# A decoder step on eight cores, rewritten from stages with barriers to 512-token tiles as concurrent threads

## The chip, the cores and the metric

One Trainium2 chip, one program on all 8 cores; each core computes one prompt of 2,048 tokens and four samples of 8 tokens with the same weights. The metric is the device time of the slowest core in microseconds (us). Such a program has a second, slower state in some executions, in which the cores of one die (0 to 3 or 4 to 7), sometimes of both, are granted a lower clock; runs marked slow are not compared.

In the later runs the slow state was so frequent (31 of the 75 runs in the experiments, of the kernel before and of the others alike) that I also compare *undisturbed cores*: of all cores of all runs of one kernel, those whose span is within 1% of that kernel's shortest span. The cores exchange nothing here, so such a core shows the kernel without the slow state. For the kernel before, this median is 3,171, 3,171 and 3,169 us on three chips, so values from different chips may be compared.

## The reference, cut to what matters

```python
def swiglu_ffn(x, w_in, w_out):
    g, u = jnp.split(x @ w_in, 2, axis=-1)
    return (jax.nn.silu(g) * u) @ w_out
# layer 0:  x += 0.5*ffn(rms(x)); x += gla(rms(x)); x += 0.5*ffn(rms(x))
# shared:   k, v = proj(rms(x)); k = rope(rms_per_head(k))
# layer 1:  x += 0.5*ffn(rms(x)); x += dilated_window_attention(rms(x), k, v); x += 0.5*ffn(rms(x))
# D_MODEL 1024, FFN 2688, GLA: 4 heads of 128 x 256 with a per-token decay, state carried from chunk to chunk
# attention: 12 query heads, 4 kv heads of 64, three groups (window, dilation) = (128,1), (512,4), (2048,16)
```

Per core this is four tiles of 512 prompt tokens (two pairs in both kernels) and one group of 32 sample tokens, each through four feed-forward blocks (FFN), one GLA (gated linear attention), one K/V projection and one attention.

## The kernel before

Everything is emitted in one program order. A stage is a list of steps, one per weight slice; every step serves both tiles of a pair (and the sample, in the first pair). The norm of a stage stands at its head, one tile after the other on one buffer, and a barrier of all engines stands at its end.

```python
def norm_to_hT(p, gcol, cvn, piece=512):
    sqb = cvn.bf([128, 8, piece]); rs = cvn.f32([128, piece])      # one buffer each
    ...
    for (c0, n) in pieces:                                        # tile after tile
        S.op(ACT, ... activation(out=sqb[:, :, 0:n], in_=xT[:, :, c0:c0 + n], func=AF.Square))   # 8 x n at once
        mm_group(PS[b][:, 0:n], [(onesb, sqb[:, fc, 0:n]) for fc in range(8)], ...)
        ...                                                       # Ln, Exp(-0.5 ..)
        for fc in range(8): S.op(DVE, ... hT = xT * gain * rs)

def ffn(p, l, f):
    emit_norm = norm_to_hT(...)
    for j in range(21):                       # step: w_in, two strips of 128 columns (512-byte rows)
        for (c0, n) in subs:                  # 512, 512 and (first pair) 32 tokens
            ...                               # 8 + 8 matmuls
            S.op(ACT, ... sg = Silu(PS[bg])); S.op(DVE, ... act = sg * PS[bu])
    for m in range(8): ...                    # step: w_out, 21 matmuls a tile, x += 0.5 * PS
    prefetch_steps(); emit_norm(); run_steps()
    S.barrier()

def gla(p):
    for (c0, n, kind) in tiles:               # one tile after the other, weights loaded for each
        step(ld(2048, 16), fn_g); ...         # gates; then v, q, k, recurrence
        step(None, fn_rec)                    # ends with S.barrier()
        ...                                   # output gates with Silu, output projection, S.barrier()
```

K is normed token by token in fp32 and transposed through the matrix engine; x and y are transposed there too. The sample's attention goes through 16 cache blocks per sequence.

Of the kernel before, what the change touches and what calls it, by code (L numbers as in the profile page):

```python
# [11 lines left out]
ENGS = ("pe", "act", "dve", "pool", "sp")  # L12
EPS = 1e-6
ds = bass.ds
# [3 lines left out]

class Sched:
    def __init__(self, nc):  # L20
        self.nc = nc
        self.sem = {e: nc.alloc_semaphore("prog_" + e) for e in ENGS}
        self.cnt = {e: 0 for e in ENGS}
        self.waited = {e: {} for e in ENGS}
        self.ops = {e: [] for e in ENGS}
        self.lastw = {}
        self.readers = {}
        self.semobj = {self.sem[e].name: self.sem[e] for e in ENGS}
        self.dma_sems = {}

    def _need(self, eng, tok, waits):
        if tok is None:
            return
        sname, val, peng = tok
        if peng == eng and peng == "pe":
            return
        if self.waited[eng].get(sname, 0) >= val:
            return
        waits[sname] = max(waits.get(sname, 0), val)

    def op(self, eng, fn, reads=(), writes=(), dma=None):
        psr = [r for r in reads if isinstance(r, tuple) and r[0] in ("ps", "psbf")]
        if psr:
            reads = [r for r in reads if r not in psr]
            writes = list(writes) + psr
# [7 lines left out]
        for s, v in waits.items():  # L53
            self.waited[eng][s] = v
        if dma is None:
            self.cnt[eng] += 1
            tok = (self.sem[eng].name, self.cnt[eng], eng)
            inc = (self.sem[eng], 1)
        else:
# [6 lines left out]
            tok = (ent[0].name, ent[1], "dma:" + dma)  # L66
# [9 lines left out]
    def barrier(self, skip=("ws", "vg")):  # L76
        for e in ENGS:
            waits = []
            for o in ENGS:
                if o != e and self.cnt[o] > self.waited[e].get(self.sem[o].name, 0):  # L80
                    waits.append((self.sem[o].name, self.cnt[o]))
                    self.waited[e][self.sem[o].name] = self.cnt[o]
            for name, (sm, c) in self.dma_sems.items():
                if name.startswith(skip):
                    continue
                if c > self.waited[e].get(sm.name, 0):
                    waits.append((sm.name, c))
                    self.waited[e][sm.name] = c
            if waits:
                self.ops[e].append((waits, None, None))  # L90

    def final_wait(self, eng="sp"):
# [9 lines left out]
    def emit(self):  # L102
        nc = self.nc
        with nc.Block() as block:
# [9 lines left out]
            block.tensor(mk("pe"))  # L114
            block.scalar(mk("act"))
            block.vector(mk("dve"))
            block.gpsimd(mk("pool"))
            block.sync(mk("sp"))

C_ID, C_LE, C_GE, C_SCP, C_SCS, C_MS, C_SQ, C_SM, C_MN, C_ONE, C_BD, C_RM, C_END = 0, 128, 256, 384, 640, 672, 704, 708, 1116, 1212, 1340, 1468, 1596  # L120
DIL = ((128, 1), (512, 4), (2048, 16))

def build_consts():
    c = np.zeros((128, C_END), np.float32)
    r = np.arange(128)
    c[:, C_ID:C_ID + 128] = np.eye(128)
    c[:, C_LE:C_LE + 128] = (r[:, None] <= r[None, :])
    c[:, C_GE:C_GE + 128] = (r[:, None] >= r[None, :])
    c[:, C_SCP:C_SCP + 256] = 1.0
    c[:, C_SCP] = 0.0  # L130
    c[:, C_SCP + 128] = 0.0
    c[:, C_SCS:C_SCS + 32] = 1.0
    c[:, C_SCS:C_SCS + 32:8] = 0.0
    t = np.arange(32)
    c[:32, C_MS:C_MS + 32] = ((t[:, None] // 8 == t[None, :] // 8) & (t[:, None] <= t[None, :]))
    for s in range(4):
        c[:32, C_SQ + s] = (t // 8 == s)
    for rt in range(17):
        for g, (win, dil) in enumerate(DIL):
            for tq in range(8):  # L140
                col = C_SM + rt * 24 + g * 8 + tq
                if rt < 16:
                    R = rt * 128 + r
                    d = 2048 + tq - R
                    c[:, col] = ((d % dil == 0) & (d >= 0) & (d <= win))
    for s in range(4):
        for g, (win, dil) in enumerate(DIL):
            for tq in range(8):
                col = C_MN + s * 24 + g * 8 + tq
                d = tq - (t % 8)  # L150
                c[:32, col] = ((t // 8 == s) & (d >= 0) & (d % dil == 0))
    c[:, C_ONE:C_ONE + 128] = 1.0
    c[:, C_BD:C_BD + 128] = (r[:, None] // 64 == r[None, :] // 64)
    for m in range(128):
        if m % 64 < 32:
            c[m + 32, C_RM + m] = -1.0
        else:
            c[m - 32, C_RM + m] = 1.0
    return c

def build_rope():
    half = 32
# [3 lines left out]
    return np.stack([np.cos(ang), np.sin(ang)], axis=0).astype(np.float32)  # L166

def build(stage=99, phases=None):
# [8 lines left out]
    xp = din("xp", [2048, 1024]); xs = din("xs", [32, 1024]); st_in = din("st", [16, 128, 256])  # L177
    ck = din("ck", [4, 2048, 256]); cv = din("cv", [4, 2048, 256])
    small = din("small", [64, 128])
    knq = din("knq", [2, 64])  # L180
    ffn_in = din("ffn_w_in", [2, 2, 1024, 5376]); ffn_out = din("ffn_w_out", [2, 2, 2688, 1024])
    gla_in = din("gla_w_in", [1024, 3088]); gla_g2 = din("gla_w_gate2", [16, 512]); gla_out = din("gla_w_out", [1024, 1024])
    kv_w = din("kv_w", [1024, 512]); wq = din("attn_w_q", [1024, 768]); wo = din("attn_w_out", [768, 1024])
    consts = din("consts", [128, C_END]); rope = din("rope", [2, 128, 2080])
    y_p = dout("y_p", [2048, 1024]); y_s = dout("y_s", [32, 1024])
    stp_o = dout("stp", [4, 128, 256]); sts_o = dout("sts", [16, 128, 256])
    kp_o = dout("kp", [2048, 256]); vp_o = dout("vp", [2048, 256]); ks_o = dout("ks", [32, 256]); vs_o = dout("vs", [32, 256])

    S = Sched(nc)
    A = nc.alloc_sbuf_tensor  # L190
    TPM = 1056
    xT = A("xT", [128, 8, TPM], F32)
    hT = A("hT", [128, 8, TPM], BF16)
    NSLOT = 4
    wsl = A("wsl", [128, NSLOT, 4096], BF16)
    CF = A("CF", [128, C_END], F32)
    CB = A("CB", [128, C_END], BF16)
    G = A("G", [128, 64], F32)
    negb = A("negb", [128, 4], F32)
    KNQ = A("KNQ", [128, 2, 64], F32)  # L200
    wg2 = A("wg2", [16, 512], BF16)
    Sst = A("Sst", [128, 4, 256], F32)
    Sbf = A("Sbf", [128, 4, 256], BF16)
    KT = A("KT", [128, 2, 2048], BF16)
    KTs = A("KTs", [128, 2, 32], BF16)
    Vg = A("Vg", [128, 3, 16, 256], BF16)
    Vsn = A("Vsn", [32, 256], BF16)
    zer = A("zer", [128, 512], BF16)
    SCRW = 19100
    scr = A("scr", [128, SCRW], F32)  # L210
    PS = [nc.alloc_psum_tensor(f"ps{b}", [128, 512], F32) for b in range(8)]
    NB = 5
    LL = 5
    PBFS = [PS[6][:, :].bitcast(BF16), PS[7][:, :].bitcast(BF16)]
    bank_ctr = [0]

    bank_ring = [list(range(NB))]

    def newbank():
        ring = bank_ring[0]  # L220
        b = ring[bank_ctr[0] % len(ring)]
        bank_ctr[0] += 1
        return b

    class Carver:
        def __init__(self):
            self.off = 0

        def f32(self, shape):
            n = int(np.prod(shape[1:]))  # L230
            v = scr[:shape[0], self.off:self.off + n]
            self.off += n
            assert self.off <= SCRW, (self.off, SCRW)
            return v if len(shape) == 2 else v.rearrange(_pat(len(shape)), **_dims(shape))

        def bf(self, shape):
            n = int(np.prod(shape[1:]))
            w = (n + 1) // 2
            v = scr[:shape[0], self.off:self.off + w].bitcast(BF16)[:, 0:n]
            self.off += w  # L240
            assert self.off <= SCRW, (self.off, SCRW)
            return v if len(shape) == 2 else v.rearrange(_pat(len(shape)), **_dims(shape))

    def _pat(nd):
        names = "abcd"[:nd - 1]
        return "p (" + " ".join(names) + ") -> p " + " ".join(names)

    def _dims(shape):
        names = "abcd"[:len(shape) - 1]
        return {names[i]: int(shape[i + 1]) for i in range(len(shape) - 2)}  # L250

    SP, PL, ACT, DVE, PE = "sp", "pool", "act", "dve", "pe"
    S.op(SP, lambda e: e.dma_start(out=CF[:], in_=consts[:, :]), writes=["CF"], dma="c0")
    S.op(PL, lambda e: e.dma_start(out=CB[:], in_=consts[:, :]), writes=["CB"], dma="c1")
# [26 lines left out]
    def _rs_init():  # L281
        if "load_idx" in rs_state:
            return
# [947 lines left out]
```

## Time and profile before

| | before |
|---|---|
| time, three runs | 3,183.6 / 3,217.4 / 3,220.5 us |
| span, slowest core of the profiled run | 3,199.2 us |
| PE / ACT / DVE busy | 82% / 24% / 31% |
| granted PE clock by core | 0.878 to 0.890 |
| time of weight queue q0's packets, as share of the 16 engines' span | 58.1% |

PE is the matrix engine, PEld its weight load, ACT the activation engine, DVE the vector engine, POOL and SP issue most transfers. In a line of waits the figures are: total us, number of waits, the longest. In a timeline: start, length, engine, source line, operation, output<-input, shapes, count, and in brackets the idle time before with what ended it. The views that carry the reading are in the prediction.

### The profile page before, as it was taken

To read this page: it belongs to the slowest core of one execution; us is meant where nothing else is said; L and a number is where in the kernel's file an instruction comes from. 1 tells how busy PE (TensorE), PEld (TensorE's weight loads), DVE (VectorE), ACT (ScalarE), POOL (GpSimd) and SP (SyncE) were. 2 spreads that over 40 slices of the span, in tenths; PEclk is the share of its full clock that TensorE was granted. 3 is DMA by queue.
4 is the path that set the end of the run, shared out by engine and by line. 5 is a ranking of instruction groups with operands and counts; after the bars stand their busy time and mean duration, and the time that the engine had idled before them with its cause. 6 is when DMAs were issued, how large, how long until landed. Compare 5 with 4: busy or idle time off the path is not lost.

```text
span 3199.2 us, 43773 instructions; the slowest of 8 cores (3162.7 to 3199.2 us)
## 1 busy us (share of the span) xinstructions
PE 2633.8 (82%) x15479; PEld 1246.8 (39%) x15479; DVE 976.6 (31%) x1843; ACT 761.9 (24%) x1445; POOL 476.9 (15%) x532
## 2 busy tenths in 40 slices
PE   5997775499948995868997998686998599877998
PEld 3443332244423442443444443332443244333444
DVE  3213442321143215643213212443112411265211
ACT  2112331211032104622102111423111311164110
POOL 1210001122003210011210220000220222000220
PEclk9998887599768998759998998897998699987999
DMA  6785468678318863256784795673793389501784
GB/s 108 73 82 62 62 94 121 92 73 80 46 37 79 77 65 53 35 74 82 72 81 101 70 85 54 86 93 43 73 86 46 58 78 90 67 15 17 73 84 88
DMA packets 619875, 228.60 MB, mean 71 GB/s; under 512 B 531648, under 2 KB 613200, under 8 KB 619664
## 3 DMA queue, kind: packets, MB, share of 16 engines
q0 software_dynamic: 602464, 194.61, 58.1%
q1 hardware_dynamic: 17200, 31.20, 3.2%
q8 instruction: 130, 2.13, 0.3%
q14 instruction: 81, 0.66, 0.1%
HBM read 404.94 MB, written 15.40 MB: 131 GB/s over the span
## 4 chain that ended last, share of the span: by engine, by line
PE 74%; DVE 8%; ACT 7%; DMA 6%; issue 3%; POOL 1%; DVEq 0%; ACTq 0%; SPq 0%; POOLq 0%
PE ps L342 69%; DVE hT L441 4%; ACT scr L433 2%; DMA scr<-cv 1%; PE ps L991 1%; DMA wsl<-gla_w_in 1%; PE ps L1023 1%; DMA scr<-xp 1%; DMA sts<-scr 1%; ACT scr L803 1%; DVE scr L563 1%; DMA wsl<-ffn_w_in 1%; DVE scr L1132 1%; ACT scr L439 1%; ACT scr L802 1%
## 5 line engine op out<-in xcount | busy, mean ns | idle before, releaser
L342 PE MATMUL ps<-hT,wsl 128*128 128x512 bf16 (+2 forms) x7720 | 1429.8, 346 | 80.3 <-DVE hT L441 37.8
L342 PEld LDWEIGHTS ps<-hT,wsl 128*128 128x128 bf16 (+1 forms) x7720 | 654.3, 99 | 844.0 <-issue 150.7
L342 PE MATMUL ps<-scr,wsl 128*128 128x512 bf16 (+1 forms) x3920 | 721.3, 345 | 31.8 <-DVE scr L1132 21.0
L471 DVE TENSOR_TENSOR scr<-scr,ps 128x512 bf16<-128x512 f32 (+1 forms) x420 | 239.1, 586 | 934.8 <-PE ps L342 934.6
L342 PEld LDWEIGHTS ps<-scr,wsl 128*128 128x128 bf16 x3920 | 331.3, 99 | 420.4 <-issue 97.9
L299 POOL DMA_DIRECT2D wsl<-ffn_w_in x336 | 294.4, 879 | 1255.1 <-DMA wsl<-ffn_w_in 839.6
L469 ACT ACTIVATE scr<-ps 128x512 f32<-128x512 f32 (+1 forms) x420 | 216.9, 517 | 964.7 <-PE ps L342 964.6
L342 PE MATMUL ps<-scr,CB 128*128 128x512 bf16 (+2 forms) x464 | 145.8, 449 | 291.6 <-ACT scr L433 189.0
L441 DVE SCALAR_TENSOR_TENSOR hT<-xT,G,scr 128x512 bf16<-128x512 f32 (+2 forms) x344 | 196.3, 571 | 195.4 <-ACT scr L439 163.6
L486 DVE SCALAR_TENSOR_TENSOR xT<-ps,xT 128x512 f32<-128x512 f32 x160 | 91.7, 590 | 522.4 <-PE ps L342 522.4
L433 ACT ACTIVATE scr<-xT 128x4096 bf16<-128x4096 f32 (+2 forms) x43 | 105.3, 2449 | 560.0 <-DVE xT L486 472.2
L342 PEld LDWEIGHTS ps<-scr,CB 128*128 128x128 bf16 x464 | 48.8, 121 | 392.9 <-issue 386.9
L299 POOL DMA_DIRECT2D wsl<-ffn_w_out x64 | 89.2, 1394 | 398.4 <-PE ps L342 396.8
L342 PE MATMUL ps<-wsl,hT 128*128 128x512 bf16 (+3 forms) x408 | 92.2, 394 | 17.8 <-ACT scr L333 13.4
L333 ACT COPY scr<-ps 128x512 f32<-128x512 f32 (+4 forms) x59 | 33.3, 583 | 306.0 <-PE ps L408 158.3
L1001 ACT ACTIVATE scr<-ps 128x48 bf16<-128x48 f32 (+4 forms) x318 | 74.8, 290 | 63.7 <-PE ps L991 61.7
L299 POOL DMA_DIRECT2D wsl<-gla_w_in x35 | 30.7, 883 | 332.5 <-PE ps L342 242.7
L342 PEld LDWEIGHTS ps<-wsl,hT 128*128 128x128 bf16 (+1 forms) x408 | 44.2, 111 | 64.8 <-issue 37.6
L1006 DVE TENSOR_TENSOR scr<-scr,CB 128x96 bf16<-128x96 bf16 (+4 forms) x159 | 48.2, 303 | 50.6 <-ACT scr L1001 46.3
L1024 PE MATMUL ps<-scr,CB 128*64 128x24 bf16 (+4 forms) x636 | 56.0, 226 | 0.0
L437 ACT ACTIVATE scr<-ps 128x512 f32<-128x512 f32 (+2 forms) x43 | 19.5, 453 | 136.1 <-DVE hT L441 83.6
L751 DVE SCALAR_TENSOR_TENSOR scr<-scr,G 128x512 bf16<-128x512 f32 (+1 forms) x40 | 26.1, 652 | 67.7 <-ACT scr L748 62.3
(124 smaller groups left out, 1298.6 us busy)
## 6 DMA issues: line engine op xcount, KB each, us to landing
wsl<-ffn_w_in POOLq DMA_DIRECT2D x336, 256.0 KB, 4.9
wsl<-ffn_w_out POOLq DMA_DIRECT2D x64, 672.0 KB, 8.7
wsl<-gla_w_in POOLq DMA_DIRECT2D x30, 1024.0 KB, 12.0
wsl<-gla_w_out POOLq DMA_DIRECT2D x10, 1024.0 KB, 9.8
scr<-xp SPq DMA_DIRECT2D x16, 512.0 KB, 6.8
y_p<-scr SPq DMA_DIRECT2D x16, 512.0 KB, 4.5
scr<-rope SPq DMA_DIRECT2D x8, 512.0 KB, 3.9
scr<-ck POOLq DMA_DIRECT2D x8, 512.0 KB, 8.0
```

What stands on the lines that cost most here:

```text
L299: S.op(PL, (lambda e, o=osl, s_=src: e.dma_start(out=o, in_=s_)), writes=[("ws", sl)], dma=f"ws{sl}_{pi}")
L333: S.op(ACT, lambda e: e.copy(out=out, in_=in_), reads=reads, writes=writes)
L342: ins = e.matmul(out, lhsT=l, rhs=r, start=(start and i == 0), stop=(stop and i == n - 1), skip_group_check=skip)
L433: S.op(ACT, (lambda e, c0=c0, n=n: e.activation(out=sqb[:, :, 0:n], in_=xT[:, :, c0:c0 + n], func=AF.Square)), reads=xkeys(c0, n), writes= ...
L439: S.op(ACT, (lambda e, n=n: e.activation(out=rs[:, 0:n], in_=rs[:, 0:n], func=AF.Exp, scale=-0.5)), reads=["rs"], writes=["rs"])
L441: S.op(DVE, (lambda e, fc=fc, c0=c0, n=n: e.scalar_tensor_tensor(out=hT[:, fc, c0:c0 + n], in0=xT[:, fc, c0:c0 + n], scalar=G[:, gcol + fc ...
L469: S.op(ACT, (lambda e, bg=bg, n=n, sl=sl: e.activation(out=sg[sl][:, 0:n], in_=PS[bg][:, 0:n], func=AF.Silu)), reads=[("ps", bg)], writes= ...
L471: S.op(DVE, (lambda e, bu=bu, n=n, sl=sl, j=j, c0=c0: e.tensor_tensor(out=act[:, j, c0:c0 + n], in0=sg[sl][:, 0:n], in1=PS[bu][:, 0:n], op ...
L486: S.op(DVE, (lambda e, b=b, n=n, m=m, c0=c0: e.scalar_tensor_tensor(out=xT[:, m, c0:c0 + n], in0=PS[b][:, 0:n], scalar=0.5, in1=xT[:, m, c ...
L1001: S.op(ACT, (lambda e, pview=pview, sview=sview: e.activation(out=pview, in_=sview, func=AF.Exp, scale=0.125)), reads=[("ps", bs)], writes ...
L1006: S.op(DVE, lambda e: e.tensor_tensor(out=pall, in0=pall, in1=mask.unsqueeze(1).to_broadcast([r1_ - r0_, 4, nqq]), op=ALU.mult), reads=["C ...
L1024: ins = e.matmul(accD[hp * 64:hp * 64 + 64, j // 2, 0:nqq], lhsT=CB[r0_:r1_, C_ONE:C_ONE + 64], rhs=rhs, start=False, stop=False, skip_gro ...
```

## The change

The intent: keep the matrix engine fed by having several independent chains to choose from. Each tile (and the sample) is a Python generator, "thread", that walks through all stages. Evacuations, recurrences and attention blocks are spawned as further threads. A merger repeatedly takes the operation with the lowest estimated start, ties by rank, and appends it to its engine's program. No stage barrier is left: only semaphores for true dependencies. Weights are laid out by the host so that each unit (1 MB of fp32, 8 KB rows) is contiguous, and stream through one ring of eight such units (bf16); a unit is freed when the sample and both tiles of a pair have used it. Silu becomes Exp, Ln, Exp, so that one activation table serves the whole kernel (one table load in its trace, 26 in the one before). Squares for the next norm are taken as each eighth of x is finished. x, y, K arrive and leave feature-major. The core of the diff:

```diff
-    for j in range(21):
-        ... for (c0, n) in subs: ...
-    prefetch_steps(); emit_norm(); run_steps()
-    S.barrier()
+class Threads:
+    TIE = 0.15
+    def run(self):
+        ...
+            cands = [(S.start_of(th[3][1], th[3][3], th[3][4]), th) for th in self.live if th[3] is not None]
+            m = min(c[0] for c in cands) + self.TIE
+            th = min((c for c in cands if c[0] <= m), key=lambda c: (c[1][0], c[1][1]))[1]
+            S.op(eng, fn, reads, writes, cost, dma, nbytes)
+def c_act(n): return 0.11 + n * 0.00083          # the estimates, us
+def c_dve(n, rate=1): return 0.07 + n / (960.0 * rate)
+    def weights():                                # thread: one ring for all weights, states and caches
+        for k, u in enumerate(order):
+            ...
+            yield need(lambda over=over: all(o.left == 0 for _, _, o in over))
+            yield O(PL, ... dma_start(out=dst, in_=u.src), writes=[u.key] + [o.key for _, _, o in over], ...)
+    def tail(T, m, last):                         # behind each eighth of x
+        ...
+            yield square(T, m); done.add(("sq", T.nm, sqn, m))
+    def ffn(T, f, last):
+        for j in range(NF):
+            u = yield from use(T, "fi%d" % f, j)
+            ...                                   # 8 + 8 matmuls
+            TH.spawn(post(j, bs, g, up), T.rank - 3)   # Exp, Ln, Exp, two multiplies
+    def tile_thread(T, prev):
+        yield from load_x(T, prev)
+        yield from norm(T, 0);  yield from ffn(T, 0, False)
+        yield from norm(T, 8);  yield from (gla(T) if T.n == 512 else gla_s(T))
+        ...
+        yield from norm(T, 40); yield from ffn(T, 3, True)
+    TH.spawn(weights(), -30); ...
+    TH.spawn(tile_thread(tiles[0], None), 0);  TH.spawn(tile_thread(TS, None), TS.rank)      # TS: the sample, rank -20
+    TH.spawn(tile_thread(tiles[1], None), 10); TH.spawn(tile_thread(tiles[2], tiles[0]), 20)
+    TH.spawn(tile_thread(tiles[3], tiles[1]), 30)
```

## The prediction

> **What bounds the kernel now.** I read four views: the page, busy time by stage, the clock core by core, and the waits of the matrix engine. First the page's busy table and slices.
>
> ```profile
> PE 2633.8 (82%) x15479; PEld 1246.8 (39%) x15479; DVE 976.6 (31%) x1843; ACT 761.9 (24%) x1445; POOL 476.9 (15%) x532
> ...
> PE   5997775499948995868997998686998599877998
> ...
> PEclk9998887599768998759998998897998699987999
> ```
>
> PE is the only engine near full, but its row dips about eight times, and the clock row dips with it. So I cut the span at the stages (busy time by stretch, slowest core; last three figures: granted clock, DMA share, GB/s):
>
> ```profile
> core 5: us, PE busy (x) PEld busy (x) DVE busy (x) ACT busy (x) POOL busy (x), PEclk, DMA share, GB/s
> ...
> 330.00:604.00 274.00, 163.77 (x1040) 82.46 (x1040) 94.62 (x182) 73.17 (x129) 21.34 (x25) 0.77 0.63 95
> 604.00:625.00 21.00, 8.58 (x30) 3.02 (x31) 8.11 (x12) 11.16 (x8) 5.86 (x7) 0.58 0.64 63
> ...
> 980.00:1212.00 232.00, 231.53 (x1512) 111.29 (x1510) 47.30 (x99) 30.94 (x66) 45.30 (x47) 0.99 0.72 69
> ...
> 2808.00:2940.00 132.00, 102.43 (x816) 45.45 (x815) 83.03 (x156) 70.91 (x179) 0.00 (x0) 0.82 0.02 5
> ```
>
> The feed-forward stretch (980 to 1212) is solid at clock 0.99. The mixers, norms and K/V stages between are not: 274 us hold 164 us of slow matmul in the first GLA, the norm after it has 9 in 21. Two pieces of the chain that ended last give the rate of a solid stretch:
>
> ```profile
> 979.80 231.75 PE ps L342 x1512
> ...
> 2964.34 216.69 PE ps L342 x992
> ```
>
> The second is 512 columns only: 216.69 / 992 = 218.4 ns each. The first is 1008 of those (220.1 us), which leaves 11.6 us for 504 of 32 columns, 23 ns each. With these rates, and the estimates of the next part for 128 and 256 columns, the program before (9,924 matmuls of 512 columns, 344 of 256, 1,522 of 128, 3,689 smaller) is about 2,380 us of matmul. The other 820 of 3,199 us are PE waiting or at half clock. The waits of PE name who it waits for:
>
> ```profile
> PE ps L342 <- ACT scr L433: 189.0, 43, 8.8
> PE ps L342 <- ACT scr L735: 52.9, 20, 8.7
> PE ps L342 <- DVE hT L441: 37.8, 10, 10.0
> ```
>
> They are the squares of the norms, the squares of the GLA norm and the normalized activations: the serial head of a stage, with no other work to lie under it.
>
> [...] nearly all solid stretches run at 1.00 on all eight cores, but two cores at a time fall to 0.81 at the end of some.
>
> ```profile
> 800.00:860.00 60.00, 60.00 (x325) 26.40 (x324) 7.41 (x16) 0.00 (x0) 4.18 (x3) 0.81 0.36 35
> 1000.00:1060.00 60.00, 60.00 (x393) 28.93 (x392) 12.02 (x25) 11.41 (x25) 15.75 (x18) 1.00 0.80 78
> ```
>
> Core 5 is at 0.81 from 800 to 860 in the second feed-forward; cores 6 and 7 are from about 215 to 290. Over all windows of 10 us in which PE is full, cores 4 to 7 have 9 to 15 of about 190 at 0.83 or less: 5 to 8%. [...] Exp and Ln follow each other with no load, and its 26 loads of 1283 ns stand at changes from or to Silu and others.
>
> **The change part by part.**
>
> *PE work.* The instruction order of the built changed kernel has 9,616 matmuls of 512 columns, 910 of 256, 862 of 128 and 3,440 of 64 columns or fewer: 9,616 x 0.2184 = 2,100; 910 x 0.109 = 99; 862 x 0.056 = 48; 3,440 x about 0.024 = 83. Sum 2,330 us, 50 less than before: the fp32 transposes of x, y and K go to the host's layouts, the zeroing matmuls of attention and half the sample's cache blocks go away. This saving is small; the gain has to come from the 820 us.
>
> *ACT.* Silu becomes Exp, Ln, Exp and two multiplies in place of one. ACT in 512-column feed-forwards goes from 336 x 0.597 = 201 us to 336 x (0.597 + 0.630 + 0.630) = 624; the GLA's 32 output gates likewise (32 x 1.26 = 40 more). Counting all forms of the order by durations of the same forms before (597 ns from PSUM, 630 ns from SBUF, 229 and 198 ns at 32 columns), ACT is some 1,230 us against 762. The table loads (33 us) go.
>
> *DVE.* 336 more multiplies of 0.688 us, less the transposes' copies: some 1,170 us against 977.
>
> Neither is the bound: for one feed-forward step of 16 matmuls PE needs 3.49 us, ACT 1.86, DVE 1.38. A PSUM pair stays taken about 3.5 us of filling plus a chain of about 4 us (three ACT, two DVE, semaphores); four pairs give one step per about 2 us, still under 3.49.
>
> *Weights.* 336 issues of two column strips (512-byte rows) become 168 of 8 KB rows through one ring of eight such units; GLA weights are read per pair of tiles, not per tile. Before, weights cost PE under 40 us of waits, so this buys little but leaves DMA room.
>
> *The stages.* No barriers: a second tile's matmuls stand in the order between the first tile's last matmul of one stage and its first of the next. I went through the order at each join and compared the PE work there with the chain that has to lie under it (evacuation 0.69, square 0.63, Ln 0.60, Exp 0.63, eight applications of 0.75: about 9 us with semaphores). My estimates of what stays open:
> - start: 13 us of loading, squares, norm, before the first full-size matmul: 28 us (62 us before);
> - feed-forward joins: the ones-matmul stands right behind the last output matmul and waits about 2 us, then 3 to 9 us of other work for a chain of 8: 3 us each, five per tile, four tiles: 60;
> - GLA: about 150 us of PE work per pair against some 120 ACT and 115 DVE, with a recurrence chain of 3 to 4 us per chunk and stretches of the order that hold only small matmuls: 35 in the first pair (with the sample's chain), 20 in the second;
> - attention: about 97 us of PE work per pair, DVE some 115 to 140: 45 in the first pair, with the sample's cache through the same ring, 40 in the second;
> - change of pair: y out, x in, squares, norm, about 22 us against 16.6 us of the other tile's matmuls: 12 in all;
> - end: evacuation and store of y, 6; small gaps, 1%: 20.
>
> Sum 266 us. Half clock after those gaps: 25. So 2,330 + 266 + 25 = 2,620 at full clock. For the drop to 0.81, which costs 23% while it lasts: the share of the worst core before (8%) would be 43 us; at double that, [...] 86. I take about 40 and round to 2,660.
>
> **Rivals.**
> [...] PE runs near full for 2.5 ms with ACT and DVE busier. For: both 0.81 periods above came 150 us or more into a solid stretch[...]. Against: six of eight solid stretches of core 5 end without it, at up to 230 us. If it held for half the time: 2,330 x 0.5 x 0.23 = 270 on 2,620, so 2,890; held all the time, about 3,150, near where we were.
> *ACT and DVE become the bound in mixers.* Both are near PE's load there, the merging order was made by estimates (0.535 us for 512 columns on ACT, where the trace has 0.597 to 0.630; 0.603 on DVE against 0.688), and PE takes its matmuls strictly in that order. If the estimates mislead it, the gaps double: 2,880.
> *The ring couples the tiles.* A unit is freed only when the sample and both tiles have used it; four sample states take 12,288 of 16,384 columns of it, one sample's cache 6,656. If the sample's chain holds weights back, a GLA or attention stage waits some 40 us more: 2,740.
> *Fewer gaps than I count.* If joins are hidden fully and the clock stays at 1.00: about 2,500.
>
> **Range and chances.** Centre 2,650: the sum, less a little since I may have counted some gaps twice. The low end takes the last rival, the high end a throttle for a quarter of the time with half again the gaps (2,620 + 134 + 70): 2,500 to 2,830. Slower or the same needs over 500 us beyond the sum, so the throttle nearly always on: 3% within, 1% slower.
>
> **What would show it right or wrong.** PE busy over 90% in most slices with no dips at stages; granted clock mean at about 0.95 with pairs of cores at 0.81 in a tenth or so of the time; ACT near 1,230 and DVE near 1,170 us; no table loads; PE's longest waits on DVE in attention and on the recurrence, none above some 60 us in total. Clock 0.81 over whole milliseconds means that the first rival won; dips of PE at the mixers with ACT or DVE at 90% there mean the second; PE waits on ring weights mean the third.

Where the recorded text told rules of the hardware that no trace here shows, it is cut and the cut is marked. No term of the sum is cut: 2,330 + 266 + 25 = 2,620, rounded to 2,660 with about 40 for the drop to 0.81. What it calls the estimates of the next part, 109 and 56 ns for 256 and 128 columns (99 and 48 us of the sum), lost the sentence that gave them, but the trace of the kernel before has the same lengths: on core 5 four matmuls of 256 columns take 0.60 us and two take 0.38, so 110 ns for each further one, and those of 128 columns start 56 ns apart (seven steps from 359.20 to 359.59 us). Half clock is in that trace too: after 4.8 us of idle time eight matmuls of 512 columns take 3.57 us (from 38.18, granted clock 0.50), where eight at 218.4 ns would be 1.75. How much of it would be left after the gaps, 25 us, and the doubling of the share at 0.81 were my guesses; no trace gives them. The first rival is the clock at 0.81 for much of the time.

## The result, and the profile after

| | before | after |
|---|---|---|
| median of the comparison's runs | 3,200.5 us (3,183.2 to 3,220.5) | 2,612.7 us (2,609.4 to 2,616.6) |
| ratio of fast runs, 95% interval | | 0.817 (0.812 to 0.822) |
| undisturbed cores, median (before: of the later runs) | 3,170 us | 2,607 us |
| granted clock by core, profiled run | 0.878 to 0.890 | 0.955 to 0.960 |

A ratio is the mean time of one kernel's fast runs over that of the other's fast runs of the same rounds, so not quite the ratio of the medians. The unaltered kernel was run again on a second chip (label a_again). It was 2,640 us (2,614 to 2,641) against 3,196, ratio 0.825 (0.819 to 0.832).

> The changed kernel unaltered, as the reference point on this chip for the three other runs. Every theory: 2,613 us within 0.4%, granted clock about 0.955 on every core, and hardly any solid stretch at 0.81 to 0.83.

Its undisturbed cores are at 2,609 us as expected. Its time is not, because in three of the four runs two to four cores are 20 to 30 us longer at a lower clock (0.943 to 0.948, the others 0.954 to 0.959); that is taken up below.

From the page of the changed kernel, the lines that answer to those of the kernel before: busy time, PE's busy slices, the granted clock.

```profile
PE 2365.2 (91%) x14580; PEld 1164.6 (45%) x14828; DVE 1126.8 (43%) x2012; ACT 1197.6 (46%) x2312; POOL 171.0 (7%) x320
...
PE   1999997999989997699997999978999899976999
...
PEclk9999998999999998699998999999999999987999
```

The dips are fewer and shallower, the clock row dips only with them, and PE is busy 91% instead of 82%. (248 matmul records are missing here, so I cut the stages in the second run, where all 14,828 are present.) The columns are as in the stage view in the prediction.

```profile
core 5: us, PE busy (x) PEld busy (x) DVE busy (x) ACT busy (x) POOL busy (x), PEclk, DMA share, GB/s
0.00:66.00 66.00, 11.65 (x154) 6.50 (x155) 10.55 (x35) 18.79 (x55) 8.05 (x18) 0.97 0.70 141
66.00:300.00 234.00, 234.00 (x1458) 112.83 (x1457) 86.46 (x160) 105.76 (x210) 13.72 (x26) 1.00 0.39 65
300.00:550.00 250.00, 226.44 (x1565) 122.75 (x1564) 142.85 (x285) 139.14 (x280) 18.19 (x31) 0.90 0.40 70
...
1000.00:1150.00 150.00, 115.52 (x1438) 65.83 (x1436) 92.17 (x189) 86.55 (x208) 10.99 (x20) 0.77 0.51 82
...
1340.00:1400.00 60.00, 39.12 (x179) 16.48 (x178) 15.09 (x24) 10.99 (x19) 3.17 (x6) 0.77 0.61 138
...
1600.00:1900.00 300.00, 275.90 (x1520) 139.79 (x1519) 154.82 (x250) 171.62 (x293) 18.48 (x35) 0.98 0.38 66
...
2250.00:2400.00 150.00, 115.19 (x951) 60.03 (x949) 94.41 (x159) 88.88 (x172) 6.76 (x12) 0.84 0.21 37
2400.00:2608.00 208.00, 200.70 (x930) 90.62 (x927) 68.33 (x100) 69.92 (x114) 11.08 (x21) 1.00 0.42 83
```

Length less PE busy gives the open gaps: start 54, first GLA 24, attention 34 and 35, change of pair 21, second GLA 24, last FFN 7. With the stretches left out here (22) they are 222 us. PE's longest waits in the first run of the changed kernel:

```profile
engine line waited for: us in total, times, longest us
PE pst L565 <- DVE h L581: 49.1, 16, 12.6
PE pst L565 <- DMA ring<-wfi: 36.4, 9, 5.9
PE pst L565 <- ACT h L570: 26.3, 9, 16.9
PE pst L565 <- DVE r L578: 24.1, 6, 8.8
```

The 189 us of waits for the norms' squares have become 26, nearly all at the start and the change of pair. The question for the experiments is which part of the rewrite took the 561 us (3,170 less 2,609, undisturbed cores of the later runs) away.

### The profile page after: what moved, and what is told of

The parts are those of the page before. It is cut to its first block, busy times and chain, and to the rows that moved or that the text cites. A ratio compares the mean times of both kernels' runs of the same rounds, so it can differ in the third digit from the quotient of the medians.

```text
span 2607.7 us, 41140 instructions; the slowest of 8 cores (2605.1 to 2607.7 us)
## 1 busy us (share of the span) xinstructions
PE 2365.2 (91%) x14580; PEld 1164.6 (45%) x14828; DVE 1126.8 (43%) x2012; ACT 1197.6 (46%) x2312; POOL 171.0 (7%) x320
## 4 chain that ended last, share of the span: by engine, by line
PE 81%; DVE 7%; ACT 4%; issue 4%; DMA 2%; DVEq 0%; POOL 0%; ACTq 0%; SPq 0%; POOLq 0%
PE pst L565 78%; DVE h L581 3%; ACT p L570 2%; DMA ring<-wfi 2%; DVE r L578 1%; DVE p L578 1%; ACT h L570 1%; ACT r L574 1%; DMA x<-xp 1%; PE pst L1310 0%; PE pst L1249 0%; PE pst L1271 0%; PE pst L898 0%; DVE p L581 0%; PE pst L899 0%
## 5 line engine op out<-in xcount | busy, mean ns | idle before, releaser
L565 PE MATMUL pst<-h,ring 128*128 128x512 bf16 x5989 | 1358.0, 382 | 60.4 <-DVE h L581 45.8
L565 PEld LDWEIGHTS pst<-h,ring 128*128 128x128 bf16 x6144 | 596.4, 98 | 767.2 <-issue 83.6
L565 PE MATMUL pst<-r,ring 128*128 128x512 bf16 x3057 | 693.5, 382 | 28.4 <-DVE r L578 23.7
L570 ACT ACTIVATE p<-p 128x512 f32<-128x512 f32 x856 | 538.0, 629 | 86.2 <-DVE p L734 11.1
L578 DVE TENSOR_TENSOR p<-p,pst 128x512 f32<-128x512 f32 x368 | 252.4, 686 | 601.7 <-ACT p L570 596.4
L570 ACT ACTIVATE p<-pst 128x512 f32<-128x512 f32 (+1 forms) x472 | 279.1, 593 | 488.2 <-PE pst L565 473.4
L565 PEld LDWEIGHTS pst<-r,ring 128*128 128x128 bf16 x3136 | 303.6, 98 | 387.0 <-issue 37.5
L570 ACT ACTIVATE h<-x 128x512 bf16<-128x512 f32 x192 | 118.0, 626 | 464.0 <-DVE x L581 317.5
L578 DVE TENSOR_TENSOR r<-p,pst 128x512 bf16<-128x512 f32 x336 | 231.3, 688 | 60.6 <-DVE p L578 51.0
L581 DVE SCALAR_TENSOR_TENSOR h<-x,CF,p 128x512 bf16<-128x512 f32 x224 | 153.2, 746 | 54.0 <-ACT p L570 42.7
```

What stands on the lines that cost most here:

```text
L565: ins = e.matmul(out, lhsT=l, rhs=r, start=(start and i == 0), stop=(stop and i == last), skip_group_check=skip)
L570: return O(ACT, lambda e: e.activation(out=out, in_=in_, func=func, scale=scale, bias=bias), reads, writes, c_act(n))
L578: return O(DVE, lambda e: e.tensor_tensor(out=out, in0=a, in1=b, op=op), reads, writes, c_dve(n, rate))
L581: return O(DVE, lambda e: e.scalar_tensor_tensor(out=out, in0=a, scalar=s, in1=b, op0=op0, op1=op1), reads, writes, c_dve(n))
```

## The experiments

All kernels gave correct results. Undisturbed cores, in us (how many of the cores that ran count as such):

| kernel | median | to the changed kernel |
|---|---|---|
| before | 3,170 (129 of 176) | +561 |
| changed (a_again) | 2,609 (24 of 32) | |
| stage_barriers | 2,646 (16 of 40) | +37 |
| mixers_in_turn | 2,732 (24 of 40) | +123 |
| turn_late | 2,733 (24 of 24) | +124 |
| turn_late_serial | 2,987 (12 of 24) | +378 |
| serial_only | 2,836 (22 of 24) | +227 |
| rows512 | 2,615 (36 of 40) | +6 |
| silu | 2,639 (32 of 40) | +30 |
| true_costs | 2,599 (28 of 32) | -10 |
| x_first | 2,600 (22 of 32) | -9 |
| x_both | 2,594 (18 of 32) | -15 |
| x_both_costs | 2,588 (44 of 64) | -21 |

### Putting the overlap back out, step by step

**stage_barriers.** The two tiles of a pair meet after every stage:

```diff
+        def meet(k):
+            if T.n == 512:
+                done.add(("stage", T.nm, k))
+                yield need(lambda: all(("stage", P.nm, k) in done for P in pair))
         yield from ffn(T, 0, False)
+        yield from meet(0)
         yield from norm(T, 8)
```

> The two tiles of a pair meet after each of six stages (12 meetings); the sample stays free, all else is kept. Theory (the gain is PE's idle time filled by the other tile's matmuls across the joins): each meeting exposes Ln, Exp and the first applications of both norms, 0.60 + 0.63 + 0.75 and semaphores, then 8 applications at 0.75 against matmuls at 0.22, some 8 us, and some 3 us of half clock after it: 12 x 11 = 130, so about 2,740 us (2,690 to 2,800). Rival (the gain is less work: fewer matmuls, no table loads, contiguous weights): 2,613 to 2,640 us.

Measured: 2,779 us (2,693 to 3,082), of five runs one fast (2,693) and even that with two cores at a lower clock; undisturbed cores 2,646. So +37, less than a third of the 130 that the theory said, and more than the rival's 27. A meeting looks like this (PE's timeline, core 0):

```profile
297.36 3.63 PE L565 MATMUL pst<-h,CB 128*128 128x512 bf16 x16
300.82 0.55 PE L565 MATMUL pst<-hsb,ring 128*128 128x32 bf16 x16
306.79 3.57 PE L565 MATMUL pst<-h,WLR 128*16 128x512 bf16 x8 [5.41 <-DVE h L581]
```

and the same join of the changed kernel like this:

```profile
278.04 1.68 PE L565 MATMUL pst<-h,CB 128*128 128x512 bf16 x7
...
289.89 1.89 PE L565 MATMUL pst<-h,WLR 128*16 128x512 bf16 x8
291.71 1.68 PE L565 MATMUL pst<-r,ring 128*128 128x512 bf16 x7
```

In the second there is no idle time: output matmuls of the other tile (r,ring) fill the chain of Ln, Exp and applications. In the first PE waits 5.4 us, and eight matmuls then take 3.57 us instead of 1.89, at half clock: 7 us, of which 1.7 are half clock, where I had guessed 3. Twelve such meetings would be 85 us; 37 came. The rest is not accounted for one by one; at the mixers' ends PE had gaps already, and the meeting moves a gap instead of adding one (argued, not shown). Such a meeting is also weaker than the old barrier: the sample passes it, no engine is stopped, and the two norms have buffers of their own. What the old barrier itself cost was not measured alone.

**mixers_in_turn.** In addition the second tile starts GLA, and the blocks of attention, only when the first has ended (GLA's weights are then loaded once per tile, which the cut leaves out):

```diff
+        if T.i == 1:
+            yield need(lambda: ("stage", tiles[T.t - 1].nm, 1) in done)
         yield from norm(T, 8)
         yield from (gla(T) if T.n == 512 else gla_s(T))
```

> The meetings of stage_barriers, and within GLA and within the blocks of attention the second tile starts when the first has ended (GLA weights are loaded once per tile for that, 16 more units per pair). Theory (overlap): in the kernel before, GLA of the first pair held 164 us of matmul in 274; with one tile at a time I expect some 75 us more per pair in GLA and some 30 in attention on top of stage_barriers: about 2,950 us (2,870 to 3,050), most of the way back to the kernel before. Rival (less work): within 40 us of stage_barriers, and below 2,700.

Measured: 2,765.6 us (2,746 to 2,802), ratio of fast runs to before 0.864 (0.858 to 0.870); undisturbed cores 2,732, so +86 on stage_barriers. Both theories miss: the rival by some 40 us in either of its figures, the overlap theory by over 200 from its centre. **What one tile does for the other across stages and in the mixers is worth 123 us of 561**, the second loading of GLA's weights included; inside the other stages the tiles still interleave.

**turn_late.** In addition the squares are taken in one instruction at the head of the norm:

```diff
-            yield square(T, m); done.add(("sq", T.nm, sqn, m))       # behind each eighth of x
+        yield act(T.h[:, :, :], T.x[:, :, :], AF.Square, 8 * n, ...)  # at the head of norm_stats
```

> On top of mixers_in_turn (undisturbed cores: 2,727 us) the squares of every norm are no longer taken as each eighth of x is finished, but in one instruction over 8 x 512 columns at the head of the norm, as in the kernel before. Theory (the norm's serial head was a main part of the 588 us, and early squares removed it, not the other tile): one Square of about 3.5 us and the 8 matmuls behind it, some 5 us more at each of 16 norms, and 2 to 3 us of half clock each: 2,840 us (2,800 to 2,890), with PE's waits on the squares (ACT h) at 80 us or more in total. Rival (with two tiles meeting there one covers the other): 2,725 to 2,750 us.

Measured: 2,739.5 us (2,739.2 to 2,739.8), three fast runs, ratio 0.861 (0.859 to 0.863); undisturbed cores 2,733. The rival holds in the time: 1 us lost. PE's waits on squares did rise, from 25 us to 63 (mixers_in_turn on core 0, turn_late on core 1):

```profile
PE pst L568 <- ACT h L573: 24.5, 6, 15.6
...
PE pst L568 <- ACT h L573: 62.8, 13, 20.2
```

But 25 of those 63 are at the start, where they stand in place of 33 us of waits for weights. Comparing progress, the start and the first stages run some 8 us ahead of mixers_in_turn and the rest gives it back. That head start is a side effect: with the squares out of the loading loop, all four x transfers of the first tile are issued before the second tile's (see the section on the start). So late squares cost some 8 us here, hidden by it, and the 189 us that I had read as the norm's serial head were not worth 189 us of early squares. The 2 to 3 us of half clock at each norm were a guess of mine: where I looked (core 1) eight matmuls take 3.19 us after 2.57 us of idle time and 3.49 after 4.56, instead of 1.89, so 1.3 and 1.6.

**turn_late_serial.** In addition the mixers' small chains stand in program order inside a tile:

```diff
-            TH.spawn(qkpost(hd, bs), T.rank - 4)
+            yield from qkpost(hd, bs)
...                                        # the same for recur, rpost, kpost, vpost, qpost
-        for s in range(NW):
-            TH.spawn(worker(s, work[s::NW]), T.rank - 5 + 0.1 * s)
+        yield from worker(0, work)         # attention: one block after the other
```

> On top of turn_late the mixers' own small chains go in program order inside a tile: GLA's q/k evacuation and transposes, recurrence and output gates, the K and q norms with rotary, and attention one block after the other (more serial than the kernel before, which kept three blocks in flight). Only FFN posts and the gates of GLA stay as threads. Theory (the rest of the gain is PE's idle time inside the mixers, filled by chains merged by estimated time): 48 attention blocks x 3 us, 32 norm-rotary chains x 3, 64 recurrence steps x 2.5, and some 50 elsewhere = 450: 3,200 to 3,300 us, at or past the kernel before. Rival (the rest is less work: host layouts, no transposes, no table loads): under 2,950 us.

Measured: 2,996 us in the one fast run of three (3,201 and 3,367 are slow); undisturbed cores 2,987: +254. Between the two theories: this is the largest single part, but 183 us remain to the kernel before. PE's waits (core 6):

```profile
engine line waited for: us in total, times, longest us
PE pst L568 <- DVE h L584: 100.2, 20, 8.0
PE pst L1265 <- DVE h L581: 68.0, 27, 6.0
PE pst L568 <- ACT p L573: 65.2, 30, 3.6
...
PE pst L862 <- ACT r L577: 43.6, 22, 3.5
```

L1265 is attention's second product waiting for its masked probabilities, ACT p the norm-with-rotary chains and GLA's output norm, L862 the recurrence's first product. In the changed kernel each has other work of the *same* tile over it.

Where the other 183 us are shows in a comparison by stage, from one norm's first matmul to the next one's, on core 3 of both (spans 3,162.7 and 2,971.3, difference 191):

| stage, first pair / second pair | before | turn_late_serial |
|---|---|---|
| K/V and third FFN | 345 / 322 | 287 / 267 |
| attention | 240 / 158 | 183 / 188 |
| GLA | 314 / 230 | 286 / 264 |
| last FFN with change of pair / end | 276 / 255 | 257 / 237 |
| start | 38 | 32 |
| first FFN | 251 / 242 | 258 / 241 |
| second FFN | 252 / 241 | 243 / 231 |

114 of the 191 are in the K/V stage. Before, it takes a norm in four pieces of 256 columns, norms K token-major, transposes it back in fp32, and then runs a second norm of the same x for the FFN; after, one statistic serves both gains and K stays feature-major. Most of the way from the K/V norm to the next FFN, before (to that FFN's norm):

```profile
859.00:944.00 85.00, 38.74 (x183) 21.14 (x184) 34.61 (x79) 30.43 (x62) 5.24 (x10) 0.64 0.18 43
```

and in turn_late_serial (to that FFN's first full-size matmul), columns as above:

```profile
818.00:872.00 54.00, 25.95 (x200) 14.37 (x198) 32.77 (x59) 23.68 (x47) 4.24 (x8) 0.79 0.54 102
```

In attention the first pair wins 57 (probably the sample's cache, 13 gathered blocks instead of 16 transposed ones), the second loses 31; one block at a time is more serial than the three in flight before, which fits. For that reason 254 is somewhat too much for the threads inside a tile, and 183 too little for the rest. I could not undo the layouts one by one, and no run puts the old barriers and the shared norm buffer back, so this part is located, not taken apart.

**serial_only.** The same program order inside a tile, but with everything else of the changed kernel (no meetings, early squares).

> The changed kernel with the mixers' chains in program order inside a tile (as in turn_late_serial), but tiles, sample and stages free to interleave and squares early. It tells whether the two kinds of overlap stand in for each other. Theory (they do: without in-tile threads the other tile's matmuls fill most of the waits): 2,660 to 2,720 us on undisturbed cores, far less than the 253 us that the same edit cost with the tiles in turn. Rival (they add up: each fills gaps of its own): 2,840 to 2,880 us.

Measured: 2,843 us (2,843 to 2,869), ratio 0.897 (0.892 to 0.901); undisturbed cores 2,836: +227, against +254 with tiles in turn. The rival holds (4 us under its range): **the two kinds of overlap hardly stand in for each other.** Taken in this order, the threads inside a tile are worth 227 us and the overlap of the tiles 151 (2,987 less 2,836), instead of 254 and 124. Its waits are those of turn_late_serial again (attention's second product 67.5 us in 27 waits, as there 68.0). A likely reason, not tested: both tiles are in the same mixer at the same time, so when one waits for such a chain, so does the other.

### Weights, activation table, estimates

**rows512.** The host lays the same units out as 16 (or 21) blocks of 128 columns, so a unit is read in 512-byte rows:

```diff
-    wfi = din("wfi", [4 * NF, 128, 2048])
+    wfi = din("wfi", [4 * NF, 16, 128, 128])       # read as "k p c -> p k c"; wfo and wgl likewise
```

> The changed kernel with feed-forward and GLA weights laid out by the host so that every unit is read in 512-byte rows, as in the kernel before; nothing else. Theory (weights are hidden under matmuls in both): the DMA share goes from 0.40 to 0.6 or more, the start and the change of pair lengthen by 5 to 10 us each, undisturbed cores at 2,610 to 2,630 us. Rival (contiguous units are a real part of the gain): over 2,660 us, and PE waits on ring units above 80 us (36 us now).

Measured: 2,627 us, four fast runs (2,623 to 2,628), ratio 0.826 (0.824 to 0.828); undisturbed cores 2,615, +6 on average (four cores of a run at about 2,607, four at 2,620). The theory holds. The weight queue of the changed kernel (packets, MB, share of 16 engines' time):

```profile
q0 software_dynamic: 45536, 169.75, 39.5%
```

The same of rows512:

```profile
q0 software_dynamic: 593376, 169.75, 64.5%
```

The same bytes in thirteen times the packets cost 1.6 times the engine time, and the transfers lie under matmuls either way. PE's waits for FFN units rise from 36 to 50 us.

**silu.** Silu and one multiply in the feed-forward posts:

```diff
-            yield from sigmoid(buf, g, n, [pk[0]], k)
-            yield tt(buf, buf, g, ALU.mult, n, [k, pk[0]], [k])
+            yield act(buf, g, AF.Silu, n, [pk[0]], [k])
```

> Feed-forward posts with Silu and one multiply instead of Exp, Ln, Exp and two. ACT loses 336 x 1.26 = 423 us (and the sample's 84 x 0.43 = 36), DVE 336 x 0.688 = 231 us; in exchange the table has to change between Silu and the Ln/Exp of norms, gates and attention of the other tile: I expect 80 to 150 loads of 1.28 us. Theory (neither ACT nor DVE is the bound): undisturbed cores within 20 us of 2,609. Rival (ACT's longer chain holds PSUM and the joins): 2,580 us or less. Second rival (interleaved tiles make the loads numerous, on the norms' chains): 2,640 or more.

Measured: 2,645 us (three fast runs, 2,644 to 2,645), ratio 0.831 (0.829 to 0.833); undisturbed cores 2,639: +30. Busy time:

```profile
PE 2406.8 (91%) x14828; PEld 1169.3 (44%) x14828; DVE 885.4 (34%) x1592; ACT 810.2 (31%) x1527; POOL 171.0 (6%) x320
```

and the group of table loads (busy us, mean ns, idle before):

```profile
L570 ACT ACT_TABLE_LOAD x56 | 71.8, 1283 | 44.4 <-PE pst L565 39.0 <-DMA xsb<-xs 4.8
```

ACT lost 387 us and DVE 241, and the kernel got slower, by 30 us where the theory allowed 20; the second rival is the nearest. Taking a third of ACT's work away gains nothing, which speaks against ACT and DVE as the bound; alone it doesn't settle it, because the table loads came back in the same edit. 56 loads, fewer than I expected, come back; their own time is 72 us, and progress falls behind by some 15 us in the first pair's attention and in small steps at other stages. That the loads cause it fits the places; the order changed too (the estimates of the posts changed), and I did not separate the two.

**true_costs.** The estimates set to the trace's durations:

```diff
-def c_act(n): return 0.11 + n * 0.00083
+def c_act(n): return 0.18 + n * 0.00086
-def c_dve(n, rate=1): return 0.07 + n / (960.0 * rate)
+def c_dve(n, rate=1): return 0.155 + n / (960.0 * rate)
```

The smallest matmul's estimate went from 0.0265 to 0.024 us as well.

> Only the estimates that the merging goes by are changed, to the durations in the trace: 512 columns on ACT 0.620 us (0.535 before), on DVE 0.688 (0.603). Theory (estimates 10 to 15% low on two engines with slack shift a matmul group here and there): within 10 us of 2,609. Rival (the wrong estimates put matmuls ahead of data that is not there, and cause a good part of the gaps in attention and GLA): 2,560 to 2,590 us.

Measured: 2,602.0 to 2,606.9 us in three fast runs, ratio 0.819 (0.817 to 0.821); undisturbed cores 2,599: -10, at the edge of the theory and far from the rival. The wrong estimates cost about 10 us.

### The start and the change of pair

In the changed kernel the first full-size FFN matmul stands at 66.6 us. PE's timeline of the first run:

```profile
50.01 0.59 PE L565 MATMUL pst<-hsb,ring 128*128 128x32 bf16 x16 [3.25 <-DMA ring<-wfi]
56.33 3.19 PE L565 MATMUL pst<-h,CB 128*128 128x512 bf16 x7 [5.72 <-ACT h L570]
...
66.64 8.56 PE L565 MATMUL pst<-h,ring 128*128 128x512 bf16 x29 [1.37 <-DVE h L581]
```

ACT's timeline of the same run (the squares are h<-x):

```profile
17.17 1.15 ACT L570 ACTIVATE h<-x 128x512 bf16<-128x512 f32 x2 [4.09 <-DMA x<-xp]
...
47.60 0.61 ACT L570 ACTIVATE h<-x 128x512 bf16<-128x512 f32 x1
```

Between 18 and 47.5 us ACT serves the sample's first seven posts, each of which waits for a weight unit that shares the DMA engines with x of two tiles (DMA share 1.0 from 20 to 47 us; the eight units of the first 66 us take 27.6 us to landing at the median, those of the whole run 5.7); the tile's other squares stand behind them in ACT's fixed order. x itself is late as well: the loads of the two tiles are issued by turns, and of the first tile's four pieces the second landed at 26 us and the last at 46 (issued at 3.4 and 7.2 us, 22.4 and 39.0 us to landing).

**x_first.** The fourth and later units of a pair's first FFN wait until the first tile's x has landed, and the second tile's x waits for it too (at the start of the program):

```diff
+            if u.hold:                                   # unit 3 of the pair's first FFN
+                yield need(lambda u=u: ("xl", tiles[2 * u.p].nm, 3) in done)
+                first = [xk(tiles[2 * u.p], m) for m in range(8)]
             yield O(PL, ... dma_start(out=dst, in_=u.src),
+                    reads=first,
```

> At both pair starts the ring's fourth and later weight units wait until the x of the first tile has landed, and the second tile's x waits for it too. Theory A (the late start, first feed-forward matmul of a full tile at 66 us, comes from x sharing the DMA engines with eight weight units of 1 MB and the other tile's x): that matmul moves to about 40 us, the gap at the pair change shrinks from 22 to about 14 us, and the whole takes 2,575 to 2,590 us. Theory B (the start is bound by bytes: what is won is given back as waits for the held units): 2,605 to 2,620 us, with PE's waits on ring<-wfi at 30 us or more in the first 150 us.

Measured: 2,608 us in the profiled run and 2,630 in the other fast one, two of four slow, ratio 0.821 (0.812 to 0.829); undisturbed cores 2,600: -9, between A and B. A's mechanism is there: the first full-size FFN matmul moved to 41 us, and at the change of pair PE waits 9 us for squares instead of 17. But part of the win at the start, and all of it at the change of pair, came back (PE's timeline, core 5):

```profile
84.45 16.68 PE L570 MATMUL pst<-h,ring 128*128 128x512 bf16 x64 [7.12 <-DVE h L586]
...
1362.78 3.57 PE L570 MATMUL pst<-h,CB 128*128 128x512 bf16 x8 [8.56 <-ACT h L575]
1373.59 25.90 PE L570 MATMUL pst<-h,ring 128*128 128x512 bf16 x112 [7.24 <-DVE h L586]
...
1408.34 62.03 PE L570 MATMUL pst<-h,ring 128*128 128x512 bf16 x273 [7.12 <-DVE h L586]
```

The first tile has used up all units that the ring holds, eight at the start (8 x 3.5 = 28 us) and seven at the change of pair (112 matmuls), before the second one's norm is done. No unit is freed, and PE waits for the second tile's norm: the ring's coupling, in neither theory. At the change of pair the three waits add up to 23 us, against 21 in the changed kernel, so nothing was won there. The win is at the start: in the first 130 us PE is idle for 44 us instead of 54 (core 5 of both). B's sign, waits for units of 30 us or more, did not come: they fell from 33 us to 21.

turn_late had such an early start without holding any weights back. Its norm stands at

```profile
31.60 3.44 PE L568 MATMUL pst<-h,CB 128*128 128x512 bf16 x8 [20.25 <-ACT h L573]
```

so all of the first tile's x had landed by then (its last piece at 28 us) beside the eight units. Bandwidth alone is thus not what made the start late. But turn_late changed two orders at once: that of the loads, in which the first tile's x comes before the second one's, and that of ACT, in which no post of the sample stands before the square. x_first changed both too. Which of the two weighs more was not tested.

**x_both.** The sixth and later units wait for the second tile's x as well:

```diff
+        u.hold = (1 if i == 3 else 2 if i == 5 else 0) if kind == "fi0" else 0
```

> As x_first, with the second tile's x ahead of the sixth and later weight units at both pair starts, so that its norm is done before the first tile has used the eight units that the ring holds. In x_first the first tile stood still at 75 us and at 1,399 us for the second one's norm, some 9 us each. Theory: both stops go, undisturbed cores at 2,580 to 2,588 us. Rival (byte-bound start: the stop comes back as a wait for held units): 2,595 us or more, with over 25 us of PE waits on ring<-wfi in the first 150 us.

Measured: one fast run of four, 2,600 us; undisturbed cores 2,594 (2,587 to 2,613): -15. That lies between the theory's 2,588 and the rival's 2,595, nearer to the rival. In the profiled run (a slow one, cores 0 and 1 undisturbed) the stop at 84 us shrank to 3.7, and the waits for units in the first 150 us are 20 us, under the rival's 25. But the second stop, which the theory had go as well, is still there: 7.3 us at the change of pair, on all eight cores. There x_both wins nothing either (21 us of waits on core 0).

**x_both_costs.** x_both and true_costs together.

> x_both and true_costs together, as the version meant to beat both kernels. On undisturbed cores true_costs took 11 us and x_both 17 us off the changed kernel's 2,609. Theory (they act in different places, the start and pair change and the mixers): 2,581 us (2,575 to 2,590) on undisturbed cores, fast runs at 2,585 to 2,595. Rival (the truer estimates already order the first matmuls better, so the two overlap): 2,590 to 2,598.

Measured: 2,595.2 and 2,595.6 us in the two fast runs of eight (median of all 2,646), undisturbed cores 2,588, inside the theory's range, though only 2 us from the rival's. It beats the kernel before by 18% and the changed one by 0.8% on undisturbed cores, and is the fastest version that I have.

No ring of another size was run. By my reckoning one of half the size would lock up (sample attention's 6,656 columns of cache and the tiles' output weights would wait on each other). So the ring's size is not tested beyond the stops above.

## Why the prediction was right or wrong

The time was right (2,650 predicted, 2,613 measured), the sum nearly so, and its parts can be checked. One step, the attribution of the gain, was wrong. That the sum came so close is in part luck: joins and small gaps were 58 us too high, the mixers 23, the clock 9, and the start and the change of pair 35 too low.

- **PE work, 2,330 us.** In the second run's core 5, 2,608.3 us of span less 221.8 idle leaves 2,386.5 busy: 56 above the count at full speed. I had 25 for half clock and 40 for the drop to 0.81. That run has no such drop, so the term "half clock" was too small by half (it also holds errors of the rates), and the other one was zero there.
- **ACT 1,230 and DVE 1,170.** 1,198 and 1,127. One table load is left of 26. "Neither is the bound" fits silu (387 and 241 us less, and slower) and the busy shares of 46% and 43%.
- **The gaps, 266.** 222 in all:

| term | predicted | measured |
|---|---|---|
| start | 28 | 54 |
| FFN joins and small gaps | 60 + 20 | 22, with 8 of them at the first pair's K/V |
| GLA | 35 + 20 | 24 + 24 |
| attention | 45 + 40 | 34 + 35 |
| change of pair | 12 | 21 |
| end | 6 | 7, with the last FFN |

- **The start** failed as a step: I counted the chain of loading, squares and norm (28 us) as if it had the engines to itself. It shares them with the second tile's x, whose loads alternate with its own, and it stands behind the sample's posts in ACT's order, which wait for weights. The **change of pair** failed alike: 17 us of wait for squares. With x ahead of the weights that wait fell to 9 us, but the second tile's norm then held PE for 7.
- **The joins** were mis-sized the other way: 3 us each, where the join shown above has none. I took the ones-matmul for a fixed wait, but the squares before it were done.
- **"The gain has to come from the 820 us", by "the stages. No barriers".** The total was right; the mechanism that I named in that step, a second tile's matmuls between the first one's stages, is worth 37 us across the joins and 86 within the mixers. 254 came from threads *inside* a tile, which I had only as estimates of what stays open (227 and 151 for the tiles in the other order). Some 183 remain with all of that put back. They lie in the places of the stage table, K/V above all; 50 of them are the matmul count by my reckoning, and how the rest divides between shorter work and the old barriers stays open. I read the waits on squares (189 us) as heads "with no other work to lie under"; turn_late puts late squares back for some 8 us with two tiles meeting.
- **Weights "buys little".** 6 us for contiguous units against 512-byte rows. The GLA weights loaded per tile were only tried together with the order of the tiles.
- **Rival 1, the clock at 0.81 for much of the time.** It did not win; the drop is rare and short in fast runs. I took it for a share of the time, from the worst core before; it comes in episodes (last section); one of 150 us costs a core some 28 us, and by their times none came in the first four runs and one on some cores in three of the four runs of a_again. The 8% was misread too: of core 7's 15 windows only seven (220 to 290 us) are such an episode, the others (0.50 to 0.83) belong to stretches at half clock or their ends.
- **Rival 2, misleading estimates.** True to 10 us. The wide gaps in attention stay with the right estimates.
- **Rival 3, the ring.** Not 40 us in the mixers (35 of the 36 us of waits for FFN units are at the start), but it is what limits the two starts once x comes earlier: stops of 9 us (start) and 7 us (change of pair) in x_first.
- **Rival 4, fewer gaps.** Right for the joins, not for the start.
- **Slips in the recorded text.** Half again the gaps is 133 us, not 70, so the high end by its own terms is 2,887, not 2,830. Of the sample's cache 13 of 16 blocks remain, not half. And PE's longest waits are on the norms' applied activations (49 us) and on weight units (36), not in attention and the recurrence.

## What to carry to other kernels

When a rewrite removes barriers and adds threads at once, put each back alone: here a meeting of the tiles at every stage cost only 37 of 561 us, while putting each tile's small chains in program order cost 227 to 254. An engine with slack can take more work (here 387 us more on ACT, in place of 56 table loads, was a gain of 30), but the order of each engine's queue is a resource: a ready operation behind one that waits for a transfer waits too (a square whose x had landed at 26 us stood until 47.6). A shared ring lets the first user run ahead only by its length, so at the start the second user's chain has to be ready within that time.

## What the traces show of the granted clock

- In the first four runs of the changed kernel all eight cores are dense for most of 2.5 ms, and in the profiled one of these only 1 to 4 of about 195 full 10-us windows per core are at 0.83 or less. Where 0.81 comes, it comes for one pair of cores or all four of a die, and lasts some 60 us (before, core 5, from 800) to 150 us (mixers_in_turn, core 4, from 2,540 to 2,690; cores 5 to 7 have theirs within 10 us of these times). It can end under the same load: core 4 there is at 0.81 in the window from 2,680 and at 1.00 in the one from 2,700, with PE busy for over 9.9 of 10 us in both. Core 2 of x_both's slow run, before, in and after one:

```profile
1400.00:1450.00 50.00, 35.44 (x145) 14.81 (x144) 20.59 (x31) 19.29 (x32) 1.29 (x3) 0.80 0.26 40
1460.00:1600.00 140.00, 140.00 (x535) 58.02 (x534) 43.14 (x63) 55.56 (x91) 7.39 (x14) 0.81 0.38 62
1620.00:1740.00 120.00, 117.15 (x720) 65.91 (x719) 50.46 (x83) 52.27 (x91) 7.39 (x14) 1.00 0.40 63
```

  I read the first line's 0.80, with PE busy for 35.4 of 50 us, as half clock after the change of pair, not as this. 150 us at 0.81 cost 150 x 0.19 = 28 us, an estimate that fits the pairs of cores that are 20 to 30 us longer in a_again. What starts an episode stays open.
- Whole runs are slow as well: 31 of 75 were here, the worst with dies at a mean clock of 0.75 and 0.78 (3,613 us instead of 3,170 for the kernel before), many of them milder. The 0.81 of the first point, held for a whole run, is the nearest candidate: it would take the changed kernel's mean of 0.957 to about 0.78 (an estimate, 0.957 x 0.81), and the slow die in x_first's slow runs had 0.79 to 0.82. No trace of so slow a run was kept, so this stays open.
